# A reordered front and mixer, and inverse roots by Newton's iteration on VectorE

## The chip, the cores and the metric

The kernel runs on one NeuronCore of a Trainium2 chip. A core has five engines with a queue of instructions each: TensorE (PE, matrix products; its weight loads are shown as PEld), VectorE (DVE), ScalarE (ACT), GpSimd (POOL) and SyncE (SP, which mostly starts transfers). Transfers run on 16 DMA engines that all queues share. The metric is the device time of one execution in microseconds.

## The reference

It is one step of a decoder layer for 512 prompt tokens and 32 sample tokens (8 requests of 4). One input projection feeds two groups of heads: retention (q, k, v and a gate; a state of 128 x 128 per head is carried over chunks of 128 tokens) and a causal depthwise convolution of width 31. Both are normed, joined and projected (the mixer); then comes a layer norm. The second half retrieves, for each token and each of 8 heads, 16 of 16384 single-neuron experts by product keys. Cut to what matters:

```python
x = layer_norm(ALPHA * x + mix, ln1_g, ln1_b)           # mix = [silu(g) * head_norm(o), conv_out] @ w_out
q = (x @ w_query).reshape(T, 8, 256)                    # two halves of 128 a head
s1, s2 = q1 . sub_keys_1, q2 . sub_keys_2               # 128 keys each
v1, i1 = top_k(s1, 16); v2, i2 = top_k(s2, 16)
sv, ci = top_k(v1[:, None] + v2[None, :], 16)           # 16 experts a head
gate = softmax(sv); act = gelu(peer_u[idx] . x)
ffn = sum(gate * act * peer_v[idx])
y = layer_norm(ALPHA * x + ffn, ln2_g, ln2_b)
```

Every norm needs 1 / sqrt(var + 1e-5): head norms four values a token, layer norms one.

## The kernel before, in words

All arithmetic is float32 but for the gate tables. The tokens stand in groups: 128 lead tokens, then 416 others (32 samples, a prompt group "b" of 128, and 256 further tokens).

The **lead** goes first through the whole front: projections, `rope`, `conv`, `conv_norm`, retention (`scores`, `attend`, `head_norm`, `gate_heads`), the mixer (`mix_mm`, `mix_norm`) and `retrieve`, the top-k of its queries. After that its 128 gathers can start (`gather`, L568 to L587): a gather fetches 128 rows of 8 KB, one per token, by GpSimd (L573); VectorE takes the dot product with the token (L576), ScalarE the gelu and the weight (L580, L581), and VectorE adds the weighted row to an accumulator (L586). Three buffers hold gathers, and a fourth takes each fourth one.

Beside these gathers runs the **front of the others**: `glu`, `conv` (half on TensorE, half on VectorE, L269), the value projection, `rope` of q and k, three retention chunks, `conv_norm`, then the mixer. In the mixer `mix_a` makes the products of a token group and `mix_b` its layer norm, the transposes to columns (L487) and, for the first two groups, a copy to DRAM (L738). The tokens' columns are `x1T`. `caches` then writes the convolution caches (ten transfers).

Then come the **remaining queries**: four units of 32 products each (two heads a unit, 416 columns wide, L803), their top-k in `retrieve` (its first operation on VectorE is L504), and beside them the **expert scores** (`scores_of`, L781 to L788): for each of 128 blocks of 128 experts, 512 KB are loaded (L784) and multiplied with 256 token columns. Scores of 76 blocks are kept before the gate tables are built (`build`, `first_keys`). At the end `v_stage` multiplies the tables with the experts' other rows (L919, L925, the banks `pB`), while 160 gathers for the samples and group "b" run beside it, and two layer norms close the kernel. The 256 loads of expert blocks alternate between the queues of SyncE and ScalarE (`turns`, L774).

What sets the order of the work: the program is written in the order above, but a scheduler then gives each engine a fixed order of its own by an estimated timeline, with the program order as priority; operations of gathers, norms and projections are interleaved by it. On the chip each engine works its list in order and waits for semaphores. Buffers are rings of tiles: the weights have four of 1 MB (`wp`), the expert blocks four of 512 KB (`uvp`). PSUM has eight banks; in the front five belong to `ps` and three to `ps0`.

An inverse root (`rsqrt`, L182) is two operations of GpSimd: an addition of epsilon and a power of -0.5. GpSimd starts the gathers too. There are 15 such roots: five head norms and ten layer norms.

Of the kernel before, what the change touches and what calls it, by code (L numbers as in the profile page):

```python
# [20 lines left out]
D = 1024  # L21
# [73 lines left out]
def tile_step(ctx: ExitStack, tc: tile.TileContext, a, o):  # L95
# [14 lines left out]
    ps = front.enter_context(tc.tile_pool(name="ps", bufs=5, space=PSUM, reuse_waits="tile"))  # L110
    ps0 = front.enter_context(tc.tile_pool(name="ps0", bufs=3, space=PSUM, reuse_waits="tile"))
# [65 lines left out]
    mhalf = per.tile([128, 1], F32, name="mhalf")  # L177
    G.memset(mhalf, -0.5)
# [3 lines left out]
    def rsqrt(dst, var):  # L182

        G.tensor_scalar(dst, var, EPS, None, op0=OP.add)
        G.tensor_tensor(dst, dst, mhalf[:dst.shape[0]].to_broadcast(list(dst.shape)), op=OP.pow)
# [56 lines left out]
    def silu_gate(w, xT, n, outs, table):  # L242
        for m in range(4):
# [41 lines left out]
    def conv_norm(y, n):  # L285
# [10 lines left out]
        rs = small("ropeB", [128, 416], bufs=1)  # L296
# [21 lines left out]
    def head_norm(po, n, kind):  # L318
# [12 lines left out]
        on = small("on", [128, 512])  # L331
# [11 lines left out]
    def k_tokens(kT, c0, n, kind):  # L343
        pt = mmps()
        kt = small("ktok", [128, 512], bufs=1)
# [7 lines left out]
    def scores(qT, kT, c0):  # L353
# [3 lines left out]
        sc = small("sc", [128, 512])  # L357
# [289 lines left out]
    lastk = rope(load_win(1), 1, xT0, 160, 0, both(k0, kS))  # L647
    conv_norm(y0, 128)
# [3 lines left out]
    silu_gate(load_win(3), xT0, 160, both(g0, gS), True)  # L652
# [101 lines left out]
    for _ in range(KX):  # L754
        next(gather0)
# [277 lines left out]
```

## Time and profile before

| | us |
|---|---|
| three runs | 1593.02, 1601.89, 1602.20 |
| median | 1601.89 |
| the profiled execution | 1610.35 |
| its span in the profile | 1608.6 |
| TensorE busy in it | 1481.2 |
| VectorE busy in it | 1223.1 |

Times in the profile are microseconds from the start of the span. A row of the timeline gives the start, the duration, the engine, the line, the operation, what it writes and reads, how often, and in brackets how long the engine was idle before it and what ended that. A row of the table of groups gives the count, the busy time, the mean duration in ns, and the idle time before the group with what ended it. A row of the table of stretches gives the stretch, its length, the busy time of TensorE, its weight loads, VectorE, ScalarE and GpSimd with the number of instructions, the granted TensorE clock, the share of the DMA engines that was busy, and GB/s.

### The profile page before, as it was taken

How to read it: one execution, taken by the hardware profiler on the slowest of the kernel's cores; microseconds unless marked ns; L12 is line 12 of the kernel's file. 1: busy time of each engine (PE TensorE's matmuls, PEld its weight loads, DVE VectorE, ACT ScalarE, POOL GpSimd, SP SyncE). 2: the span in 40 equal slices, each digit the busy share in tenths (PEclk: the TensorE clock that was granted, in tenths of full speed). 3: DMA queues.
4: the chain of work that ended last, by engine and by line, in shares of the span. 5: the costliest groups of instructions: out<-in, count | busy, mean ns of one | idle time of the engine just before them, and what ended most of it. 6: DMA issues, size and time to landing. Idle time of an engine off the chain costs nothing.

```text
span 1608.6 us, 20726 instructions
## 1 busy us (share of the span) xinstructions
PE 1481.2 (92%) x7014; PEld 1016.0 (63%) x7014; DVE 1223.1 (76%) x3158; ACT 601.6 (37%) x1687; POOL 394.4 (25%) x335
## 2 busy tenths in 40 slices
PE   6899989996879997999999997989999999999997
PEld 6788557554666666888888885434566655644443
DVE  3939989989774999999866989667777677776642
ACT  2225352244221323333623799512994111111100
POOL 1001323433431222221122100233223223333200
PEclk9999989997989999999999997999999999999999
DMA  9458678997789768998699721989999999999972
GB/s 356 178 200 350 247 252 294 345 356 253 262 338 360 254 232 311 351 333 313 221 390 375 282 80 58 374 344 417 375 350 387 418 406 420 416 423 424 425 263 94
DMA packets 99542, 503.75 MB, mean 313 GB/s; under 512 B 10183, under 2 KB 21191, under 8 KB 56549
## 3 DMA queue, kind: packets, MB, share of 16 engines
q0 software_dynamic: 42240, 305.12, 48.9%
q1 hardware_dynamic: 32317, 122.84, 20.5%
q10 hardware_dynamic: 24880, 74.47, 12.4%
q8 instruction: 55, 0.90, 0.2%
q14 instruction: 50, 0.41, 0.1%
HBM read 497.03 MB, written 5.80 MB: 313 GB/s over the span
## 4 chain that ended last, share of the span: by engine, by line
PE 32%; DMA 28%; DVE 20%; issue 12%; POOL 5%; ACT 2%; ACTq 0%; POOLq 0%; SPq 0%; DVEq 0%
DMA g<-in_uv_dram,Ib 15%; PE pB L925 12%; PE sp L787 9%; DMA g<-in_uv_dram,I 8%; DVE acc L586 5%; PE mm L199 5%; POOL g L573 4%; DVE g L576 3%; PE mm L878 2%; DMA uv<-in_uv_dram 2%; DMA g<-in_w_in_dram 2%; DVE score L506 1%; PE mm L309 1%; PE mm L476 1%; DVE iu L505 1%
## 5 line engine op out<-in xcount | busy, mean ns | idle before, releaser
L787 PE MATMUL sp<-x1T,uv 128*128 128x256 f32 x2048 | 465.9, 383 | 25.4 <-DMA uv<-in_ut_dram 13.1
L787 PEld LDWEIGHTS sp<-x1T,uv 128*128 128x128 f32 x2048 | 386.0, 191 | 99.1 <-issue 27.7
L586 DVE SCALAR_TENSOR_TENSOR acc<-g,wgt,acc 128x1024 f32<-128x1024 f32 x285 | 364.8, 1280 | 102.1 <-ACT wgt L581 101.3
L573 POOL DMA_INDIRECT g<-in_uv_dram,I x128 | 177.1, 1384 | 451.9 <-DVE acc L586 253.5
L580 ACT ACTIVATE act<-act 128x1 f32<-128x1 f32 x288 | 57.8, 201 | 611.5 <-DVE g L576 599.9
L573 POOL DMA_INDIRECT g<-in_uv_dram,Ib x128 | 158.2, 1236 | 431.7 <-DVE acc L586 238.0
L576 DVE SCALAR_TENSOR_TENSOR g<-g,x1g 128x1024 f32<-128x1024 f32 x160 | 195.6, 1224 | 89.1 <-DMA g<-in_uv_dram,Ib 60.5
L576 DVE SCALAR_TENSOR_TENSOR g<-g,x 128x1024 f32<-128x1024 f32 x128 | 155.4, 1215 | 38.2 <-DMA g<-in_uv_dram,I 38.0
L199 PE MATMUL mm<-x1T,w 128*128 128x384 f32 (+1 forms) x512 | 177.6, 503 | 0.0
L925 PE MATMUL pB<-uv,Ga 128*128 128x512 f32 x352 | 157.2, 594 | 4.5 <-DMA uv<-in_uv_dram 4.4
L865 ACT ACTIVATE off<-row,e1T 128x128 bf16<-128x128 bf16 x512 | 157.7, 388 | 1.6 <-PE sp L787 0.6
L199 PEld LDWEIGHTS mm<-x1T,w 128*128 128x128 f32 x512 | 97.5, 192 | 71.9 <-issue 39.5
L925 PE MATMUL pB<-uv,Gb 128*128 128x512 f32 x256 | 117.4, 613 | 6.1 <-DMA uv<-in_uv_dram 5.6
L925 PEld LDWEIGHTS pB<-uv,Ga 128*128 128x128 f32 x352 | 66.3, 190 | 77.2 <-issue 67.4
L925 PE MATMUL pB<-uv,Gd 128*128 128x512 f32 x256 | 111.0, 593 | 2.9 <-DMA uv<-in_uv_dram 2.9
L925 PEld LDWEIGHTS pB<-uv,Gd 128*128 128x128 f32 x256 | 48.3, 190 | 65.4 <-issue 60.5
L925 PEld LDWEIGHTS pB<-uv,Gb 128*128 128x128 f32 x256 | 48.7, 196 | 64.2 <-issue 55.3
L878 PEld LDWEIGHTS <-A 128*128 128x128 bf16 x1536 | 64.4, 99 | 35.3 <-issue 26.3
L878 PE MATMUL mm<-B,A 128*128 128x96 bf16 (+1 forms) x1536 | 67.8, 196 | 11.6 <-DVE Gc L904 10.0
L873 DVE TENSOR_TENSOR B<-M,gtT 128x768 bf16<-128x768 bf16 (+1 forms) x192 | 69.5, 418 | 11.6 <-PE mm L878 11.6
L925 PE MATMUL pB<-uv,Gc 128*128 128x512 f32 x160 | 73.0, 601 | 0.0
L867 ACT ACTIVATE A<-off 128x1024 bf16<-128x1024 bf16 x64 | 67.4, 1053 | 14.4 <-PE mm L878 10.3
(279 smaller groups left out, 1701.5 us busy)
## 6 DMA issues: line engine op xcount, KB each, us to landing
uv<-in_ut_dram ACTq DMA_DIRECT2D x80, 512.0 KB
uv<-in_uv_dram SPq DMA_DIRECT2D x80, 512.0 KB
uv<-in_ut_dram SPq DMA_DIRECT2D x48, 512.0 KB
uv<-in_uv_dram ACTq DMA_DIRECT2D x48, 512.0 KB
w<-in_w_in_dram SPq DMA_DIRECT2D x18, 1024.0 KB
w<-in_w_query_dram SPq DMA_DIRECT2D x16, 1024.0 KB
w<-in_w_out_dram SPq DMA_DIRECT2D x7, 1024.0 KB
g<-in_uv_dram,I POOLq DMA_INDIRECT x128, 8.0
```

Source lines behind the costliest of these rows:

```text
L199: T.matmul(p[:, :n], w[m // 2][:, k, (m % 2) * 128:(m % 2 + 1) * 128], xT[:, k, c0:c0 + n], start=(k == 0), stop=(k == 7))
L309: mm = T.matmul(p[:n, q * 256:(q + 1) * 256], xT[:, k, c0:c0 + n], w[q][:, k, :], start=(k == 0), stop=(k == 7))
L573: G.indirect_dma_start(out=t, out_offset=None, in_=a["uv"], in_offset=bass.IndirectOffsetOnAxis(ap=idx[:, k:k + 1], axis=0))
L576: dot = V.scalar_tensor_tensor(t[:, :D], t[:, :D], 1.0, x1, op0=OP.mult, op1=OP.mult, accum_out=act[:, 0:1])
L580: S.activation(act[:, 1:2], act[:, 0:1], AF.Gelu)
L586: V.scalar_tensor_tensor(acc, v, wgt, acc, op0=OP.mult, op1=OP.add)
L787: T.matmul(sp, u[:, k], x1T[:, k, NG2:], start=(k == 0), stop=(k == 7))
L865: S.activation(off[:, t], row, AF.Abs, bias=e1T[:, t1 + t:t1 + t + 1])
L867: S.activation(A, off, AF.Relu, bias=1.0, scale=-1.0)
L873: V.tensor_tensor(B[:, q], M, pairs_of(gtT[:, q], t1).to_broadcast([128, TB // 2, ne, 2]), op=OP.mult)
L878: T.matmul(pt[:, t % nt], A[:, t - t1], B[:, q, (t - t1) // 2, :, t % 2], start=(q == 0), stop=(q == 2))
L925: T.matmul(pB[b][q], W[:, b * 128:(b + 1) * 128], vt[:, q * 512:(q + 1) * 512], start=False, stop=(e == NK - 1), skip_group_check=True)
```

## The change

Four things are changed.

1. `rsqrt` runs on VectorE: epsilon is added, a first guess is made by integer operations on the float's bits, and three rounds of Newton's iteration follow, three operations each, 12 in all. GpSimd's two operations go.
2. The front is reordered. In the lead the gate projection stands ahead of `conv_norm`. For the others, `conv_norm` and `caches` stand ahead of the projection of k; scores and tokens of k are made for all three chunks first, into free tiles; then each chunk's `attend`, `advance` and `head_norm` follow one of four parts of the gate projection. The third block of output weights goes into the convolution's buffer and the second of query weights into the buffer of q and k.
3. The mixer gets four new PSUM banks (`mx`), and the first query unit four others (`pq`). That unit is computed in three passes over its columns, as the token groups are normed, and no longer after the mixer. The norm of the first prompt group stands ahead of the products of the second, not behind them.
4. All loads of expert blocks are in SyncE's queue.

```diff
+    fps = ExitStack()
+    ps = fps.enter_context(tc.tile_pool(name="ps", bufs=5, space=PSUM, reuse_waits="tile"))
+    ps0 = fps.enter_context(tc.tile_pool(name="ps0", bufs=3, space=PSUM, reuse_waits="tile"))
...
     def rsqrt(dst, var):
-        G.tensor_scalar(dst, var, EPS, None, op0=OP.add)
-        G.tensor_tensor(dst, dst, mhalf[:dst.shape[0]].to_broadcast(list(dst.shape)), op=OP.pow)
+        tmp = gw.tile([128, 2, H], F32, name="nwt")
+        x, t = (tmp[:dst.shape[0], i, 0:dst.shape[1]] for i in range(2))
+        V.tensor_scalar(x, var, EPS, None, op0=OP.add)
+        V.tensor_scalar(dst.bitcast(I32), x.bitcast(I32), 1, None, op0=OP.logical_shift_right)
+        V.tensor_scalar(dst.bitcast(I32), dst.bitcast(I32), -1, 0x5F3759DF, op0=OP.mult, op1=OP.add)
+        for _ in range(3):
+            V.tensor_tensor(t, dst, dst, op=OP.mult)
+            V.scalar_tensor_tensor(t, t, -0.5, x, op0=OP.mult, op1=OP.mult)
+            V.scalar_tensor_tensor(dst, t, 1.5, dst, op0=OP.add, op1=OP.mult)
...
+    silu_gate(load_win(3), xT0, 160, both(g0, gS), True)
     conv_norm(y0, 128)
     sc = scores(q0, k0, 0)
     po = attend(0, sc, q0, v0, 0)
     on = head_norm(po, C, "p")
-    silu_gate(load_win(3), xT0, 160, both(g0, gS), True)
     gate_heads(on, C, g0, 0)
...
-    rope(load_win(1), 1, xT, n - NS, 160, [(0, n - NS, kT)])
-    wg = load_win(3)
-    banks[:] = [ps0]
-    ons = {}
-    def retain(c):
-        c0 = C * (c - 1)
-        sc = scores(qT, kT, c0)
-        kt = k_tokens(kT, c0, C, "p")
-        po = attend(c, sc, qT, vs[c], c0)
-        advance(c, kt, vs[c])
-        ons[c] = head_norm(po, C, "p")
-    retain(1)
-    retain(2)
-    banks[:] = [ps]
-    silu_gate(wg, xT, n - NS, [(0, n - NS, gT[:, :, r])], False)
-    wo = load_w(a["w_out"], 0) + load_w(a["w_out"], 512)
+    wk_, wg = load_win(1), load_win(3)
     S.activation(y[:, :, s_], yS, AF.Copy)
     conv_norm(y, n)
+    caches()
+    rope(wk_, 1, xT, n - NS, 160, [(0, n - NS, kT)])
+    spare = [u_p.rearrange("p m t -> p (m t)")[:, 0:2 * D], blk[:, 0:2 * D]]
+    spare = [t.rearrange("p (k e) -> p k e", k=8) for t in spare]
+    wo = load_w(a["w_out"], 0) + load_w(a["w_out"], 512, [spare[0], None])
+    banks[:] = [ps0, ps]
+    flat = lambda t: t.rearrange("p a b -> p (a b)")
+    scs = [None, None, flat(small("qe", [128, 4, 128], bufs=1))]
+    kts = [None] + [flat(small("dg", [128, 4, 128])) for _ in range(2)]
+    for c in range(3):
+        scs[c] = scores(qT, kT, C * c, scs[c])
+        kts[c] = k_tokens(kT, C * c, C, "p", kts[c])
+    ons = {}
+    gate_part = lambda m: silu_gate(wg, xT, n - NS, [(0, n - NS, gT[:, :, r])], False, [m])
     S.activation(gT[:, :, s_], gS, AF.Copy)
-    banks[:] = [ps, ps, ps0, ps, ps0, ps, ps, ps0]
+    for c in range(1, 4):
+        gate_part(c - 1)
+        po = attend(c, scs[c - 1], qT, vs[c], C * (c - 1))
+        advance(c, kts[c - 1], vs[c])
+        ons[c] = head_norm(po, C, "p", bv[0] if c == 3 else None)
+    gate_part(3)
+    wq0 = load_w(a["w_query"], 0, [None, spare[1]])
...
-    gate_heads(ons[1], C, gT, NS)
-    gate_heads(ons[2], C, gT, NS + C)
-    retain(3)
-    gate_heads(ons[3], C, gT, NS + 2 * C)
+    for c in range(1, 4):
+        gate_heads(ons[c], C, gT, NS + C * (c - 1))
+    fps.close()
+    leftp, mxs = ExitStack(), ExitStack()
+    pq = leftp.enter_context(tc.tile_pool(name="pq", bufs=4, space=PSUM, side="right", reuse_waits="tile"))
+    mx = mxs.enter_context(tc.tile_pool(name="mx", bufs=4, space=PSUM, reuse_waits="tile"))
+    banks[:] = [mx]
+    q_first = [pq.tile([128, 512], F32, name="mm") for _ in range(4)]
+    def first_unit(c0, c1):
+        for m in range(4):
+            for k in range(8):
+                T.matmul(q_first[m][:, c0:c1], wq0[m // 2][:, k, (m % 2) * 128:(m % 2 + 1) * 128], x1T[:, k, c0:c1],
+                         start=(k == 0), stop=(k == 7), skip_group_check=True)
     mix_a(0, NS, None)
     mix_a(NS, C, 0)
     mix_b(0, NS)
+    mix_b(NS, C)
     mix_a(NS + C, C, 1)
-    mix_b(NS, C)
     mix_a(NS + 2 * C, C, None)
+    first_unit(0, NS + C)
     mix_b(NS + C, C)
+    first_unit(NS + C, NS + 2 * C)
     mix_b(NS + 2 * C, C)
-    caches()
+    first_unit(NS + 2 * C, n)
...
-        next(turns).dma_start(u, a["ut"][e])
+        nc.sync.dma_start(u, a["ut"][e])
...
-        w = load_w(a["w_query"], h0 * 256)
+        w = load_w(a["w_query"], h0 * 256) if h0 else None
         for m in range(4):
-            S.activation(qs[:, h0 * 2 + m], project(w, m, x1T, 0, n), AF.Copy)
+            S.activation(qs[:, h0 * 2 + m], project(w, m, x1T, 0, n) if h0 else q_first[m][:, :n], AF.Copy)
...
-        next(turns).dma_start(vt, a["uv"][e * NK:(e + 1) * NK, D:])
+        nc.sync.dma_start(vt, a["uv"][e * NK:(e + 1) * NK, D:])
```

More of the change, by code (lines that the diff above doesn't have):

```diff
@@ L1 @@
 from contextlib import ExitStack
-from itertools import cycle
 import numpy as np
@@ L240, in glu, with silu_gate @@
                                        sg[:, c].rearrange("p (b i) -> p b i", b=SB), op0=OP.add, op1=OP.mult)
-    def silu_gate(w, xT, n, outs, table):
-        for m in range(4):
+    def silu_gate(w, xT, n, outs, table, blocks=range(4)):
+        for m in blocks:
             p = project(w, m, xT, 0, n)
@@ L295, in conv_norm @@
             T.matmul(pv[:, :n], onesm, sq[:, :n], start=(m == 0), stop=(m == 3))
-        rs = small("ropeB", [128, 416], bufs=1)
+        rs = small("sg", [128, 416], bufs=1)
         S.activation(rs[:, :n], pv[:, :n], AF.Sqrt, bias=eps_c)
@@ L330, in head_norm @@
         V.scalar_tensor_tensor(nb[:n], mv[:n, :, 0], -1.0, rs[:n], op0=OP.mult, op1=OP.mult)
-        on = small("on", [128, 512])
+        if on is None:
+            on = small("on", [128, 512])
         for h in range(H):
@@ L351, in k_tokens, with scores @@
         return kt
-    def scores(qT, kT, c0):
+    def scores(qT, kT, c0, sc=None):
         pa = mmps()
@@ L755, in tile_step @@
         next(gather0)
+    mxs.close()
     front.close()
@@ L765, in tile_step @@
     sel[0] = left.enter_context(tc.tile_pool(name="sel", bufs=2))
-    leftp = ExitStack()
-    pq = leftp.enter_context(tc.tile_pool(name="pq", bufs=4, space=PSUM, reuse_waits="tile"))
     banks[:] = [pq]
```

15 lines of the change are left out of this document (6 added, 9 removed).

## The prediction

> **What bounds the kernel now.** I read the busy line of the page first, then a table of stretches that I cut where the work changes: the lead chunk, the retrieval of that chunk with the convolution, the stretch M (rest of the front and the mixer), the remaining queries, the expert scores, the building of gate tables, the products with gathers beside them, and the end.
>
> ```profile
> span 1608.6 us, 20726 instructions
> PE 1481.2 (92%) x7014; PEld 1016.0 (63%) x7014; DVE 1223.1 (76%) x3158; ACT 601.6 (37%) x1687; POOL 394.4 (25%) x335
> core 0: us, PE busy (x) PEld busy (x) DVE busy (x) ACT busy (x) POOL busy (x), PEclk, DMA share, GB/s
> 0.00:111.00 111.00, 89.40 (x528) 79.96 (x528) 67.58 (x272) 25.83 (x64) 10.12 (x21) 0.95 0.65 242
> 111.00:312.40 201.40, 190.87 (x863) 133.41 (x862) 175.89 (x503) 79.83 (x210) 60.80 (x40) 0.97 0.82 295
> 312.40:515.90 203.50, 170.48 (x734) 122.83 (x733) 151.51 (x247) 67.08 (x168) 68.57 (x59) 0.91 0.84 315
> 515.90:810.00 294.10, 279.17 (x1251) 219.76 (x1250) 278.48 (x1090) 110.71 (x279) 66.06 (x53) 0.99 0.79 288
> 810.00:875.00 65.00, 64.86 (x319) 56.66 (x319) 38.82 (x52) 14.28 (x51) 14.59 (x14) 1.00 1.01 403
> 875.00:1050.00 175.00, 162.47 (x1242) 119.48 (x1242) 146.13 (x455) 137.34 (x385) 19.41 (x18) 0.94 0.56 205
> 1050.00:1531.00 481.00, 458.51 (x1934) 255.06 (x1933) 341.24 (x507) 160.45 (x523) 151.61 (x124) 0.99 0.99 402
> 1531.00:1608.60 77.60, 65.47 (x152) 28.79 (x152) 23.43 (x36) 6.12 (x13) 3.28 (x7) 0.96 0.48 170
> ```
>
> TensorE is busy for 1481 of 1609 us, and its work is nearly the same in both kernels. So the time is that work plus TensorE's idle time, 127 us in all, and the change is worth what it does to those 127. They lie at 21.6 us in the lead, 10.5 to the end of the convolution, 33.0 in M, 15.1 up to 875 us, 12.5 in the building, 22.5 beside the gathers and 12.1 at the end. From 810 to 875 us TensorE is busy 64.86 of 65 us: it is what the gate tables wait for, so a delay of TensorE before that point passes on whole.
>
> M runs from the last convolution operation on VectorE to the first top-k operation of the remaining queries (of the rows with an arrow, the numbers are the total wait in us, how many, the longest):
>
> ```profile
> 311.80 0.60 DVE L269 SCALAR_TENSOR_TENSOR blk<-u_p,cols,blk 128x384 f32<-128x384 f32 x1
> 515.95 0.29 DVE L504 MAX8 vf<-score 128x8 f32<-128x128 f32 x1 [5.53 <-ACT score L525]
> PE mm L340 <- ACT on L333: 13.3, 2, 11.8
> PE mm L487 <- DVE xr L456: 10.5, 1, 10.5
> PE mm L487 <- DVE lrs L452: 5.9, 1, 5.9
> 478.52 22.71 PE L199 MATMUL mm<-x1T,w 128*128 128x416 f32 x64
> 501.08 13.98 PE L787 MATMUL sp<-x1T,uv 128*128 128x256 f32 x64
> ```
>
> The waits of TensorE in M are for norms: 13.3 us for a head norm, 10.5 and 5.9 for layer norms. These are the holes that the change is aimed at. After them come the first query unit (22.71 us) and 13.98 us of expert scores, in which VectorE has little to do.
>
> **The change, part by part.**
>
> *The gathers in M.* The scheduler writes a fixed order for each engine, and VectorE's order holds the two operations of every expert gather (a dot product and an accumulation) between the operations of the norms. In the emitted orders, M holds 44 dots and 46 accumulations before, and 61 and 62 in the changed kernel: 95 dots instead of 80 are ahead of the first top-k. The mixer waits for VectorE in that order, so their cost counts.
>
> ```profile
> L586 DVE SCALAR_TENSOR_TENSOR acc<-g,wgt,acc 128x1024 f32<-128x1024 f32 x46 | 58.8, 1278 | 17.9 <-ACT wgt L581 17.5
> L576 DVE SCALAR_TENSOR_TENSOR g<-g,x 128x1024 f32<-128x1024 f32 x44 | 53.5, 1218 | 21.9 <-DMA g<-in_uv_dram,I 21.9
> DVE acc L586 <- ACT wgt L581: 17.5, 12, 8.7
> DVE lrs L452 <- POOL lrs L185: 5.3, 3, 2.2
> 359.87 0.16 DVE L326 TENSOR_TENSOR hrs<-hmv,cst 128x4 f32<-128x4 f32 x1
> 359.95 0.61 DVE L253 SCALAR_TENSOR_TENSOR blk<-mm,cols,sg 128x384 f32<-128x384 f32 x1
> 71.59 0.29 DVE L282 TENSOR_TENSOR tap_s<-u_s,cols 128x128 f32<-128x128 f32 x1
> 71.91 0.29 DVE L283 TENSOR_TENSOR samples<-samples,tap_s 128x128 f32<-128x128 f32 x1
> ```
>
> A tiny operation keeps VectorE for 0.08 us of its 0.16 when the next one does not need its result (359.87 to 359.95). With the same overlap a dot costs 1.14 us and an accumulation 1.20. The extra work is 17 x 1.14 + 16 x 1.20 = 38.6 us.
>
> *Newton's iteration.* Each inverse root was two GpSimd operations and is now 12 tiny ones on VectorE; 92 of them stand in M. At 0.08 us that is 7.4 us; if each had to wait for the one before, as the pair at 71.59 and 71.91 does at 0.32 us apart, 29 us. I take 7.4, since the order puts gather operations and other norms between most of them, and keep the other end for the range. What goes is the 5.3 us for which VectorE waited on GpSimd, and GpSimd's queue now holds gathers alone.
>
> VectorE's work in M is then 151.5 + 38.6 + 7.4 = 197.5 us, against 203.5 us that M lasts today. VectorE idled 39.8 us beside the gathers in M; without one wait of 8.7 us for ScalarE, that is 0.7 us for each of the 44. Zero idle gives 197.5 us, 0.7 for each of 61 gathers gives 240. I take 0.5, as the denser order has fewer other norms to wait for but the same four gather buffers: M = 197.5 + 30.5 = 228 us, **24.5 us longer**.
>
> *First query unit by columns.* It becomes three passes over the same weights, with 160, 128 and 128 columns, and starts while later token groups are still being normed. Such narrow products stand in the lead:
>
> ```profile
> 80.75 7.70 PE L199 MATMUL mm<-g,w 128*128 128x160 f32 x48
> 111.10 2.05 PE L199 MATMUL mm<-g,w 128*128 128x128 f32 x16
> ```
>
> The wide pass has 64 records. The narrow ones make 64 x 0.160 + 128 x 0.128 = 26.7 us, 4 more than the 22.7 in M today. I add nothing, because without the scores TensorE has 170.5 - 14 = 156.5 us of work in M and 228 - 156.5 = 71 us of holes; uncovered it would be the 4. With only four PSUM banks left for the mixer, the norm of the first prompt group now stands directly ahead of the next product, where it was covered by half a product. What M no longer holds are the 13.98 us of expert scores: in the emitted order the first top-k products follow the query unit at once. That work comes later, on TensorE, **14 us**.
>
> *Lead and convolution.* The gate projection (32 products) moves ahead of the convolution norm, where TensorE waited for VectorE:
>
> ```profile
> PE mm L209 <- DVE ropeB L211: 3.6, 2, 3.4
> PE mm L289 <- DVE g L269: 2.0, 1, 2.0
> ```
>
> That can return up to 5.6 us; I take 4, as two Newton roots (24 operations, 2 us or more) join that chain. From there to M, VectorE has two gathers fewer ahead of it, about 5 us in a stretch where it is 87% busy; I take 4. Together **-8**, bounds 0 and -12.
>
> *After M.* VectorE has 15 gathers (35 us) fewer between 516 and 810 us, and the 80 expert loads that stood in ScalarE's queue go to SyncE's. TensorE's waits there are
>
> ```profile
> PE sp L787 <- ACT Ga L833: 9.7, 5, 3.7
> PE sp L787 <- ACT Gb L838: 2.4, 3, 0.9
> ACT qs L803 <- DMA out_dram<-on: 10.1, 1, 10.1
> ```
>
> I take **-8** of those 12.1, bounds 0 and -15. The ten cache outputs, issued earlier on SyncE, no longer hold the query copies for 10.1 us; TensorE was doing scores meanwhile, so by itself this is worth nothing. On SyncE they now stand among the output-projection loads, with the third block waiting for the convolution buffer; these loads have the whole retention to land, and I cost them at nothing. Without that cover the mixer would wait for one load of 1 MB, some 3 us at 315 GB/s. The half of the query weights that goes into the query buffer waits for the last chunk's products, which precede the mixer by 60 us of TensorE work: nothing. The 48 expert-row loads that join SyncE are weighed among the rivals.
>
> *The end.* Two norms follow the last product:
>
> ```profile
> 1595.81 0.21 DVE L449 BATCH_NORM_AGGREGATE lmv<-lst 128x2 f32<-128x12 f32 x1
> 1597.41 0.14 DVE L452 SCALAR_TENSOR_TENSOR lrs<-lmv,lrs 128x1 f32<-128x1 f32 x1
> ```
>
> From statistics to scale took 1.6 us through GpSimd; twelve operations take 1.0 to 3.9 us by the two spacings above. I take **+1** (bounds -0.5 and +3).
>
> **Sum**: -8 + 24.5 + 14 - 8 + 1 = +23.5 us. The profiled execution took 1610.35 us, span 1608.6; it would take 1634. The runs shown have a median of 1601.89 (1593 to 1602), so I forecast **1625 us**. A change of under 1%, 16 us, cannot be told from none by a measurement of this kernel.
>
> **The rivals.**
>
> *VectorE keeps pace.* If gathers land early enough that VectorE hardly idles in M, M is 197.5 us and the sum is -8 - 6 + 14 - 8 + 1 = -7: **1595 us**. It speaks for this that GpSimd issues gathers as soon as a buffer is free; against it, that VectorE idled 52 us in M with fewer gathers. The order breaks even at 204.5 us, 3.35 us a gather.
>
> *The loads are the gain, and the kernel is faster.* Beside the gathers TensorE waits 21.1 us for expert loads:
>
> ```profile
> PE pB L925 <- DMA uv<-in_uv_dram: 10.8, 8, 4.0
> PE sp L787 <- DMA uv<-in_ut_dram: 10.3, 9, 2.3
> q0 software_dynamic: 17484, 127.39, 64.4%
> q1 hardware_dynamic: 9100, 33.14, 18.0%
> q10 hardware_dynamic: 8928, 32.51, 16.8%
> ```
>
> Half of them are issued from ScalarE's queue, behind its arithmetic. If late issue is their cause, SyncE starts each as its buffer falls free and most of the 21 us go; with M at 205 us the sum is 0.5 - 17 = -17: **1585 us**, and with M at 197.5, 1578. It decides only if M stays under about 205 us. Against it: the transfer engines are 99% busy in that stretch, so the loads are late because the path is full.
>
> [...]
>
> **How the numbers follow.** Forecast 0.55, with a range of its own from 1605 to 1640 (idle of 0.2 to 0.7 us a gather, and the bounds of the other terms). VectorE keeps pace 0.20 (1587 to 1609). Faster by the loads 0.12. One queue starves 0.13. Left out of 1588 to 1655 are the faster case, a little of the second, and the top of the last, together under 0.2; dependent Newton operations, up to 22 us more, fall inside it. Slower than 1618: 0.13 and seven tenths of 0.55. Faster than 1586: 0.12 and 0.03 of the second. The rest is within 1%.
>
> **What would show it.** In the changed profile the first top-k of the remaining queries should begin near 304 + 228 = 532 us (502 if VectorE keeps pace), with 95 dots before it, TensorE some 70 us idle since the convolution, and its waits for VectorE's norms longer, not gone. From there to the gate tables TensorE should idle under 10 us. [...] I am wrong if M is under 205 us, or if TensorE's idle time before 875 us shrinks.

## The result and the profile after

The changed kernel takes **1662.62 us** (median of four runs, 1653.63 to 1667.79) against 1602.05 of the kernel before: a ratio of **1.0386, with a 95% interval of 1.0331 to 1.0441**. It is slower by 61 us of the medians, 48 of the profiled executions (1658.23 against 1610.35, spans 1656.5 and 1608.6).

The busy line of the page of the changed kernel, and its table of stretches, cut at the same events as the prediction's table:

```profile
span 1656.5 us, 21212 instructions
PE 1501.9 (91%) x7142; PEld 1022.3 (62%) x7142; DVE 1244.7 (75%) x3338; ACT 603.1 (36%) x1686; POOL 351.4 (21%) x304
core 0: us, PE busy (x) PEld busy (x) DVE busy (x) ACT busy (x) POOL busy (x), PEclk, DMA share, GB/s
0.00:111.00 111.00, 90.25 (x551) 80.38 (x552) 70.31 (x296) 27.61 (x68) 7.91 (x16) 0.97 0.67 249
111.00:302.20 191.20, 181.37 (x817) 126.04 (x816) 169.94 (x498) 73.99 (x193) 47.75 (x36) 0.97 0.81 296
302.20:554.40 252.20, 175.45 (x820) 131.14 (x821) 201.49 (x392) 75.96 (x200) 86.32 (x61) 0.80 0.81 305
554.40:790.00 235.60, 227.35 (x1013) 176.82 (x1013) 230.38 (x1029) 83.83 (x193) 39.16 (x33) 1.00 0.72 260
790.00:895.00 105.00, 102.81 (x495) 89.84 (x494) 64.69 (x89) 34.76 (x114) 26.73 (x24) 1.00 0.97 382
895.00:1070.00 175.00, 163.73 (x1289) 129.67 (x1288) 122.92 (x420) 122.44 (x350) 9.80 (x9) 0.95 0.45 159
1070.00:1580.00 510.00, 496.59 (x2019) 260.63 (x2018) 360.28 (x548) 179.04 (x559) 133.69 (x127) 0.99 1.00 396
1580.00:1656.50 76.50, 64.34 (x149) 27.77 (x147) 24.64 (x69) 5.51 (x11) 0.00 (x0) 0.95 0.42 149
```

M, from the last convolution operation to the first top-k of the remaining queries, is 252.2 us in place of 203.6. TensorE idles 76.75 us in it (before: 33.0), and its granted clock is 0.80 (before: 0.91).

| | before | predicted | after |
|---|---|---|---|
| convolution ends | 312.4 | 304 | 302.2 |
| first top-k | 516.0 | 532 | 554.4 |
| M | 203.6 | 228 | 252.2 |
| first top-k to the first operation on table Gb | 354.7 | 360.7 | 359.5 |
| from there to the end | 737.9 | 739 | 742.6 |

So the difference is M: +48.6 of 47.9 us in all. The terms around it cancel: -10.2, +4.8, +4.7.

What TensorE and VectorE waited for in M of the changed kernel (total us, how many, the longest):

```profile
PE mm L495 <- DVE keys L464: 26.1, 2, 17.3
PE mm L495 <- DVE xr L464: 12.7, 1, 12.7
PE mm L363 <- DVE blk L218: 11.6, 3, 7.2
PE mm L346 <- ACT on L339: 10.1, 1, 10.1
PE mm L346 <- ACT b_v L339: 6.7, 1, 6.7
DVE g L584 <- DMA g<-in_uv_dram,I: 37.5, 26, 5.5
```

L495 is the transposes behind a layer norm, L346 those behind a head norm: TensorE stands before norms for 55.6 of the 76.75 us, against 29.7 before. Why the norms are late is seen in VectorE's own order. These are operations of one head norm of the changed kernel (L331 takes the variance, L184 to L186 are the first three of the root, L333 uses the finished root), with some of what stands between them:

```profile
380.32 0.15 DVE L331 TENSOR_TENSOR hrs<-hmv,cst 128x4 f32<-128x4 f32 x1
...
382.70 1.23 DVE L584 SCALAR_TENSOR_TENSOR g<-g,x 128x1024 f32<-128x1024 f32 x1 [1.31 <-DMA g<-in_uv_dram,I]
...
384.05 1.28 DVE L594 SCALAR_TENSOR_TENSOR acc<-g,wgt,acc 128x1024 f32<-128x1024 f32 x1
385.24 0.17 DVE L184 TENSOR_SCALAR nwt<-hrs 128x4 f32<-128x4 f32 x1
...
386.31 1.27 DVE L594 SCALAR_TENSOR_TENSOR acc<-g,wgt,acc 128x1024 f32<-128x1024 f32 x1
387.50 0.17 DVE L185 TENSOR_SCALAR hrs<-nwt 128x4 int32<-128x4 int32 x1
...
387.86 1.20 DVE L584 SCALAR_TENSOR_TENSOR g<-g,x 128x1024 f32<-128x1024 f32 x1
388.98 0.08 DVE L584 DVE_READ_ACCUMULATOR g<-g,x 128x1 f32 x1
388.98 0.17 DVE L186 TENSOR_SCALAR hrs<-hrs 128x4 int32<-128x4 int32 x1
...
401.75 0.16 DVE L333 TENSOR_TENSOR hrs<-hrs,cst 128x4 f32<-128x4 f32 x1
```

From the variance to the use of the root it takes 21.4 us, with twelve operations of 0.16 us in between. Eleven gather operations of 1.2 us stand in nine of the thirteen gaps of this chain and fill some 13 us of it; operations of another head norm, of the gate projection (L258) and of the retention (L388), and 1.5 us of waiting for a gather, fill most of the rest. With the power, in the kernel before, the norms from 279 us on took 1.5 to 6.3 us each.

### The profile page after: what moved, and what is told of

The parts are those of the page before. It is cut to its first block, busy times and chain, and to the rows that moved or that the text cites. A ratio compares the mean times of both kernels' runs of the same rounds, so it can differ in the third digit from the quotient of the medians.

```text
span 1656.5 us, 21212 instructions
## 1 busy us (share of the span) xinstructions
PE 1501.9 (91%) x7142; PEld 1022.3 (62%) x7142; DVE 1244.7 (75%) x3338; ACT 603.1 (36%) x1686; POOL 351.4 (21%) x304
## 4 chain that ended last, share of the span: by engine, by line
PE 37%; DMA 25%; DVE 22%; issue 10%; POOL 4%; ACT 2%; SPq 0%; POOLq 0%; DVEq 0%; ACTq 0%
PE sp L808 16%; PE pB L946 13%; DMA uv<-in_ut_dram 7%; DMA g<-in_uv_dram,I 7%; DVE acc L594 5%; POOL g L581 4%; DVE g L584 4%; DMA uv<-in_uv_dram 3%; DMA g<-in_uv_dram,Ib 3%; PE mm L204 3%; PE mm L899 2%; DMA g<-in_uv_dram,Is 2%; DMA g<-in_w_in_dram 2%; PE mm L764 1%; DVE iu L513 1%
## 5 line engine op out<-in xcount | busy, mean ns | idle before, releaser
L808 PE MATMUL sp<-x1T,uv 128*128 128x256 f32 x2048 | 461.1, 381 | 14.3 <-ACT Ga L854 9.8
L581 POOL DMA_INDIRECT g<-in_uv_dram,I x128 | 171.7, 1342 | 531.8 <-DVE acc L594 235.4
L581 POOL DMA_INDIRECT g<-in_uv_dram,Ib x128 | 136.9, 1070 | 518.0 <-DVE acc L594 330.2
L946 PE MATMUL pB<-uv,Ga 128*128 128x512 f32 x352 | 162.4, 604 | 1.2
L204 PE MATMUL mm<-x1T,w 128*128 128x384 f32 (+1 forms) x448 | 157.7, 508 | 0.7 <-DVE sc L366 0.7
L204 PEld LDWEIGHTS mm<-x1T,w 128*128 128x128 f32 x448 | 86.6, 195 | 63.5 <-issue 32.6
```

The costliest lines, as they stand in the source:

```text
L204: T.matmul(p[:, :n], w[m // 2][:, k, (m % 2) * 128:(m % 2 + 1) * 128], xT[:, k, c0:c0 + n], start=(k == 0), stop=(k == 7))
L581: G.indirect_dma_start(out=t, out_offset=None, in_=a["uv"], in_offset=bass.IndirectOffsetOnAxis(ap=idx[:, k:k + 1], axis=0))
L808: T.matmul(sp, u[:, k], x1T[:, k, NG2:], start=(k == 0), stop=(k == 7))
L946: T.matmul(pB[b][q], W[:, b * 128:(b + 1) * 128], vt[:, q * 512:(q + 1) * 512], start=False, stop=(e == NK - 1), skip_group_check=True)
```

## The experiments

In the table, "norms" is the time from the variance to the operation that uses the root, summed over the four head norms and four layer norms from 279 us on; "dots" is how many gather dot products stand ahead of the first top-k in VectorE's emitted order. The kernel before had medians of 1600 to 1602 us beside these runs. M, norms and dots are of one profiled execution each; those of e4 and e5 are the slowest of their runs. M does not hold the same work everywhere: in the kernel before, e7 and e14 it has 64 products of expert scores, 14 us, which come behind it in the changed kernel, e2 to e4, e10 to e13, e15 and e16 (at most 2 are left in M there). The others have 32 to 56.

| kernel | us | ratio, 95% | M | norms | dots |
|---|---|---|---|---|---|
| before | 1602 | | 203.6 | 32 | 80 |
| changed | 1662.62 | 1.0386 (1.0331-1.0441) | 252.2 | 127 | 95 |
| e1 Newton alone | 1655.72 | 1.0341 (1.0292-1.0390) | 249.2 | 160 | 92 |
| e2 changed, power | 1635.41 | 1.0194 (1.0140-1.0248) | 216.2 | 38 | 88 |
| e3 changed, dots from 75 held | 1644.00 | 1.0268 (1.0215-1.0320) | 226.4 | 107 | 80 |
| e4 changed, dots from 61 held | 1645.73 | 1.0265 (1.0215-1.0314) | 209.4 | 92 | 66 |
| e5 Newton alone, one round | 1642.65 | 1.0244 (1.0209-1.0279) | 236.4 | 110 | 88 |
| e6 square root and reciprocal | 1624.76 | 1.0114 (1.0049-1.0180) | 207.8 | 46 | 82 |
| e7 before, one queue | 1599.55 | 0.9981 (0.9961-1.0001) | 203.4 | 32 | 80 |
| e8 before, dots from 61 held | 1600.91 | 0.9992 (0.9966-1.0018) | 180.8 | 24 | 68 |
| e9 Newton alone, guarded | 1620.81 | 1.0116 (1.0071-1.0161) | 215.9 | 88 | 80 |
| e10 changed, power, old mixer | 1613.37 | 1.0068 (1.0042-1.0093) | 206.0 | 32 | 85 |
| e11 changed, power, unit whole | 1628.27 | 1.0162 (1.0124-1.0199) | 219.5 | 34 | 89 |
| e12 as e11, old mixer order | 1614.93 | 1.0099 (1.0063-1.0134) | 205.9 | 34 | 85 |
| e13 changed, guarded | 1621.78 | 1.0137 (1.0104-1.0170) | 218.0 | 72 | 81 |
| e14 before, guarded | 1608.55 | 1.0046 (1.0023-1.0068) | 209.6 | 26 | 80 |
| e15 changed, power, guarded | 1611.77 | 1.0067 (1.0044-1.0090) | 208.4 | 23 | 80 |
| e16 as e10, guarded | 1616.89 | 1.0115 (1.0076-1.0154) | 203.6 | 25 | 80 |

**Which part costs: Newton's iteration alone (e1), and the rest without it (e2).** e1 puts the new `rsqrt` into the kernel before; e2 takes it out of the changed kernel again:

```diff
     def rsqrt(dst, var):
-        tmp = gw.tile([128, 2, H], F32, name="nwt")
...
+        G.tensor_scalar(dst, var, EPS, None, op0=OP.add)
+        G.tensor_tensor(dst, dst, mhalf[:dst.shape[0]].to_broadcast(list(dst.shape)), op=OP.pow)
```

> The kernel before with Newton's iteration alone; front, mixer and queues as before. Its emitted order has 34 dots of gathers ahead of the last convolution operation and 92 ahead of the first top-k of the remaining queries, so 58 in stretch M (44 before, 61 in the changed kernel). Theory 1, that VectorE's order with too many gathers in M makes the loss: M grows by 14 x (2.34 + 0.9) + 7 = 52 us to about 255 us, the time to 1645 to 1655 us. Theory 2, that the reordered mixer with its uncovered norms makes the loss and Newton costs only its own 92 small operations: 1605 to 1612 us.

> The changed kernel with GpSimd's power in place of Newton's iteration; the rest as changed. Its order has 36 dots ahead of M and 88 at its end, so 52 in M. Theory 1: M shrinks from 252 us by 9 x 3.3 + 7 to about 215 us, the time from 1662 to about 1625 us. Theory 2: the mixer is still the changed one, 1650 to 1658 us.

M of e1, and two of TensorE's waits in it; below them M of e2:

```profile
306.50:555.70 249.20, 176.54 (x726) 122.29 (x725) 194.59 (x383) 75.42 (x198) 90.76 (x59) 0.83 0.83 311
```

```profile
PE mm L345 <- ACT on L338: 27.0, 2, 22.7
PE mm L492 <- DVE nwt L189: 20.7, 1, 20.7
```

```profile
313.40:529.60 216.20, 168.56 (x816) 127.88 (x817) 168.48 (x270) 69.98 (x177) 82.57 (x66) 0.86 0.85 317
```

Newton's iteration alone makes the kernel 54 us slower, nearly all that the whole change does; one wait of 20.7 us is put down to an operation of the iteration itself (L189). But without it 33 us stay. In both runs M came out near theory 1 (about 255 and 215 us); the time of e2 is 10 us above it and fits neither theory. The two parts do not add up to 61: each by itself makes the mixer's norms late (the aggregate of the last one is at 512.9 us in e1, at 505.8 in e2 and at 466.2 in the kernel before).

**Is it the gathers' number in M? (e3, e4)** In the changed kernel the later dots are kept behind the mixer's last norm:

```diff
+            if x1 is x1_0 and k >= 74:
+                behind(dot, held[0])
```

In e4 the number is 60.

> The changed kernel, with the dots of gathers 75 and later kept behind the last norm of the mixer in the order. It has 34 dots ahead of M and 80 at its end: 46 in M, as many as before (44), but the mixer, its banks and Newton's iteration are the changed ones. Theory 1: M about 208 us, the time 1615 to 1625 us. Theory 2: M stays above 235 us, the time above 1645 us.

> As the run with 74, but the dots of gathers 61 and later are kept back: 32 in M, 66 ahead of the first top-k. Theory 1: M is then no longer bound by gathers but by TensorE's products and the norms, 175 to 190 us; later VectorE has 14 more gathers between the top-k operations than before, which may cost 5 to 10 us; the time 1590 to 1605 us. Theory 2: above 1645 us.

Both theories missed a part. M falls by 26 and 43 us, and the layer norms are short again (2.4 to 2.6 us in e4), but only 17 to 19 us are gained, and e4 gains no more than e3: what is put off comes back as work later (from the first top-k to the end e4 takes 1134 us, the changed kernel 1102). In both kernels the head norms are as stretched as ever (39, 22, 16 us).

**How the cost goes with the chain's length (e5, e6).** In the kernel before, one round in place of three (six operations; the roots are less exact), or a ScalarE square root and a VectorE reciprocal:

```diff
-        for _ in range(3):
+        for _ in range(1):
```

```diff
+        S.activation(dst, var, AF.Sqrt, bias=eps_c[:dst.shape[0]])
+        V.reciprocal(dst, dst)
```

> The kernel before with Newton's iteration in place of GpSimd's power, but one round in place of three: six dependent VectorE instructions a norm in place of twelve (the roots are less exact; nothing else is left out). Theory 'stretched chain': what costs is that gather instructions of about 1.2 us are put between the dependent ones, so the cost goes by their number; the stretch M, which twelve lengthened by 46 us, should grow by 18 to 28 us (222 to 232 us), and the time should come to 1622 to 1632 us. Rival 'another order': the cost is not in the chain's length but in the order that the whole kernel is given once the root leaves GpSimd; then six cost what twelve do, M near 249 us and 1650 to 1658 us.

> The kernel before with the root as one ScalarE square root and one VectorE reciprocal: GpSimd is out of the norms as with Newton's iteration, but the chain has one VectorE instruction. 'Stretched chain': the norms take 3 to 6 us each, as with the power, so M is 198 to 210 us and the time 1597 to 1610 us. 'Another order': once GpSimd is out, M is near 249 us and the time 1645 us or more.

M is 203.6, 207.8, 236.4 and 249.2 us for no, one, six and twelve dependent VectorE operations: it goes with the chain, and GpSimd's absence alone (e6) does little to M. The dots ahead of the first top-k go with it too (80, 82, 88, 92), so these runs by themselves do not part the chain's length from the number of gathers; e3 and e13 do, below. Six operations cost more than half of what twelve cost (41 us against 54), so my proportional estimate missed. The time of e6 is 15 us above the range that I had for it, though M is in its range. Of the 12.5 us between the two profiled executions 4.2 lie in M, 5.4 ahead of it and 5.5 beside the later gathers. What costs them is not shown; ScalarE is busy 634.1 us in e6 against 601.6, and 13 table loads of 1.28 us stand at the line of the square root:

```profile
L182 ACT ACT_TABLE_LOAD x13 | 16.7, 1283 | 3.3 <-DVE x L662 2.9
```

**One queue, and holding dots back in the kernel before (e7, e8).** e7 changes `next(turns).dma_start` to `nc.sync.dma_start` at both places; e8 is the edit of e4 in the kernel before.

> The kernel before with every expert load of the scoring and building stages issued by SyncE, as the changed kernel has it, and nothing else. If one queue paces the loads a little slower, as the last 610 us of the changed kernel lasting 6 us longer suggest: 1605 to 1610 us, all of the difference behind the first gate-table multiplication. The rival from the prediction, one queue starves the loads: 1615 us or more with waits for loads of 20 us. If the queue is nothing and those 6 us are the gather's: 1600 to 1603 us.

> The kernel before with the gather's dot products from the 60th on kept behind the mixer's last norm (the order alone changes). If gather instructions ahead of the mixer's norms already cost in the kernel before, and what is put off finds room later: M falls from 204 us to 185 to 193 us and the time to 1588 to 1596 us. If VectorE has no room later, as the two holds of the changed kernel suggest (17 us less of M, nothing of the time): M falls by 8 to 15 us, the scoring and building stages give it back, and the time is 1600 to 1610 us.

TensorE's waits for expert loads between the gate tables and the last dot, in the kernel before, in e7 and in the changed kernel:

```profile
PE pB L925 <- DMA uv<-in_uv_dram: 12.8, 10, 4.0
PE sp L787 <- DMA uv<-in_ut_dram: 10.3, 9, 2.3
```

```profile
PE pB L923 <- DMA uv<-in_uv_dram: 2.5, 2, 1.5
PE sp L785 <- DMA uv<-in_ut_dram: 1.7, 1, 1.7
```

```profile
PE sp L808 <- DMA uv<-in_ut_dram: 3.6, 21, 0.2
PE pB L946 <- DMA uv<-in_uv_dram: 2.0, 4, 0.8
```

One queue takes 19 us of waits away and neither costs nor wins time (0.9961 to 1.0001). e8 takes 23 us off M, more than either theory had, and wins nothing: from the first top-k to the end it takes 18 us longer. That is the second theory, that VectorE has no room later.

**The same instructions with the chains kept together (e9, e13).** An order constraint holds each dot behind the norm that it should not come ahead of. Nothing else is changed, and all twelve operations run. `roots` are the last operations of the roots in program order; in e13 the counts are 31, 48, 51, 56, 64, 67, 72, 80:

```diff
+        roots.append(end)
...
+            if x1 is x1_0 and k >= 31:
+                behind(dot, roots[max(j for j, c in {2: 31, 3: 48, 4: 51, 5: 57, 6: 64, 7: 65, 8: 69, 9: 73}.items() if c <= k)])
```

> The kernel before with Newton's iteration alone (three rounds, twelve instructions), and an order constraint: from the 31st on, the gather's dot products may not come ahead of the norms that they stand behind in the kernel before (31 ahead of the first later norm, 48, 51 and 57 ahead of the prompt's head norms, 64, 65, 69 and 73 ahead of the mixer's norms). So the same twelve instructions run, with few gather instructions between them. 'Stretched chain': the head norms take 4 to 9 us in place of 29 to 43, M is 205 to 220 us and the time 1605 to 1622 us. If Newton's own work or the loss of GpSimd's order is what costs: M over 235 us and 1640 us or more.

> The changed kernel whole, Newton's iteration in it, with the order constraint on the gather's dot products alone (31 ahead of the first later norm, 48, 51 and 56 ahead of the head norms, 64, 67, 72 and 80 ahead of the mixer's). If the stretched chains are what Newton's iteration costs here too, it comes to what the changed kernel gives with the power back, 1635 us, and something for the chains that stay partly stretched (the same constraint on the kernel before left 18 us): 1632 to 1648 us, M 214 to 232 us. If something else in the iteration costs: M over 240 us and 1652 us or more.

M of e13, and the head norm of the same chunk as above (the first, the last and some of its twelve operations):

```profile
296.60:514.60 218.00, 170.42 (x831) 127.52 (x831) 176.91 (x358) 68.36 (x177) 61.36 (x48) 0.87 0.79 299
```

```profile
366.58 0.16 DVE L334 TENSOR_TENSOR hrs<-hmv,cst 128x4 f32<-128x4 f32 x1
366.77 0.17 DVE L186 TENSOR_SCALAR nwt<-hrs 128x4 f32<-128x4 f32 x1
366.98 0.17 DVE L187 TENSOR_SCALAR hrs<-nwt 128x4 int32<-128x4 int32 x1
...
368.76 0.16 DVE L191 SCALAR_TENSOR_TENSOR nwt<-nwt 128x4 f32<-128x4 f32 x1
368.96 0.16 DVE L192 SCALAR_TENSOR_TENSOR hrs<-nwt,hrs 128x4 f32<-128x4 f32 x1
```

With nothing between them the twelve take 2.4 us in place of 16.5 (385.24 to 401.72 in the changed kernel). Three dots follow them here, so from the variance to the use of the root it is 5.9 us in place of 21.4. The constraint wins 35 us for Newton's iteration alone and 41 for the whole change; e13 came out 10 us under the range that I had for it. But the expectation of e9 was missed in one point: its head norms take 6.9 to 22 us, not 4 to 9, so the chains are kept together only in part.

e3 is the fair comparison for the reason. It has as many dots ahead of the top-k as e13 (80 and 81) and layer norms as long in sum (22 us both), but head norms of 84 us in place of 50, and it takes 22 us longer. In the two profiled executions 8.3 of 23.3 us of this lie in M, 7.8 ahead of it and 5.7 beside the later gathers, so it is not shown that the norms make all of it.

**Controls (e14, e15): the same constraint with the power.** Here the dots stand behind the first VectorE operation that uses the root.

> The kernel before, power and all, with the order constraint of the guarded Newton kernel (31, 48, 51, 57, 64, 65, 69, 73), here ahead of the first VectorE operation that uses the root. It is the control of that run: what the constraint does without Newton's iteration. If the constraint helped there only by keeping gather instructions out of Newton's chains: 1596 to 1604 us here, and the whole 35 us there belong to the chains. If spreading the gather thinner helps by itself: 1570 to 1590 us, and Newton's part is larger than the 18 us that stayed.

> The changed kernel with GpSimd's power back and the same order constraint as the guarded changed kernel (31, 48, 51, 56, 64, 67, 72, 80). If the constraint also helps the reordered mixer, whose norms wait for VectorE directly: 1605 to 1618 us, M near 205 us, and Newton's iteration with guarded chains costs some 5 to 15 us. If it helps Newton's chains only: 1630 to 1638 us as without it; then Newton's iteration, guarded, would be no cost, but a gain of 10 us.

e14 is slower than both of its theories had it: in the old order the constraint by itself costs 6.5 us. e15 is where its first theory had it: in the changed order the constraint wins 24 us without Newton's iteration.

| us | gathers free | gathers guarded |
|---|---|---|
| before | 1602.05 | 1608.55 |
| before, Newton | 1655.72 | 1620.81 |
| changed, power | 1635.41 | 1611.77 |
| changed (Newton) | 1662.62 | 1621.78 |

With the gathers guarded (the counts differ a little between the two orders), Newton's iteration costs 12 us in the old order and 10 in the new one, and the rest of the change 3 and 1. With the gathers free the same parts cost 54 and 27, 33 and 7. So most of the loss is neither in the new instructions nor in the new order of the stages, but in where the scheduler puts gather instructions once a norm's chain has gaps or the mixer leaves VectorE waiting. The constraint moves gathers out of the chains and out of M alike (80 and 81 dots in place of 88 to 95), and the square does not part the two. The guarded chains are still not all short (88 and 72 us of norms, against 26 and 23), so the 10 to 12 us are no clean price of the iteration.

**What of the reordering costs (e10, e11, e12).** All three are e2 with more of the mixer undone: e10 has the whole old mixer (eight banks, old order, query unit behind it), e11 only the unit whole, e12 the unit whole and the old order, with the four banks kept. This is the edit of e12:

```diff
     mix_b(0, NS)
-    mix_b(NS, C)
     mix_a(NS + C, C, 1)
+    mix_b(NS, C)
     mix_a(NS + 2 * C, C, None)
-    first_unit(0, NS + C)
     mix_b(NS + C, C)
-    first_unit(NS + C, NS + 2 * C)
     mix_b(NS + 2 * C, C)
-    first_unit(NS + 2 * C, n)
+    first_unit(0, n)
```

> The changed kernel with GpSimd's power back, and its mixer as in the kernel before: eight PSUM banks for it in place of four, the old order of its four blocks, and the first query unit whole behind it, from weights loaded there. What stays of the change is the front's order (gates between the heads' blocks, scores and keys ahead, cache writes early) and the one queue. Theory 'mixer': the 34 us that stayed with the power back come from the four banks and the columns: 1600 to 1612 us. Theory 'front': they come from the front's order: 1625 to 1640 us, with the conv end to the first mixer norm as long as with the power back alone (116 us).

> The changed kernel with GpSimd's power back and the first query unit computed whole behind the mixer's last norm, from the weights and into the banks that the change gives it; only the column pieces are undone (192 matmuls of 128 to 160 columns, 27 us with the power back, in place of 64 of 416). If the pieces cost by their own work: TensorE's busy time falls by 5 us and the time is 1626 to 1632 us. If they pay by filling the wait for the mixer's norms: M grows by 10 to 20 us and the time is 1640 to 1655 us.

> The changed kernel with GpSimd's power back, the first query unit whole, and the mixer's four blocks in the old order; the four PSUM banks for the mixer stay, and so do the front and the one queue. It stands between the run with the unit whole (1628 us, M 219.5 us) and the one with the old mixer altogether (1613 us, M 206 us). Theory 'order': what cost those 15 us is that two blocks' matmuls stand ahead of the third norm: 1611 to 1618 us. Theory 'banks': it is the four banks for eight: 1625 to 1631 us.

It is the order: 13 us between the medians of e11 and e12 (their slowest and fastest runs, 1619.12 and 1627.08 us, are still 8 apart), nothing more for the banks (1614.93 and 1613.37, intervals overlapping). The statistics of the mixer's norms in e11 and e12 (first and last start):

```profile
L451 DVE BATCH_NORM_STATS2 lst<-mm x6: 678/690/694, 429.6 to 489.9; 128x6 f32<-128x512 f32 x6
```

```profile
L451 DVE BATCH_NORM_STATS2 lst<-mm x6: 678/688/693, 429.4 to 474.1; 128x6 f32<-128x512 f32 x6
```

The first begins at the same time; the last is 16 us later in e11. TensorE's rows show where these 16 us arise, first e11, then e12:

```profile
445.37 1.09 PE L490 MATMUL mm<-cst,keys 128*128 128x128 f32 x4 [13.53 <-DVE keys L459]
```

```profile
447.73 1.04 PE L490 MATMUL mm<-cst,keys 128*128 128x128 f32 x8
```

These are the transposes of the first prompt group. In the new order they stand ahead of the products of the second group, and TensorE waits 13.5 us for their norm; in the old order those products fill the wait. So it is this wait, and not the products of two groups ahead of the third norm, as my theory had it. Of the 13 us it can be all; four more dots (89, against 85) stand ahead of the first top-k in e11 too. The column pieces by themselves are 7 us, with overlapping intervals, so not told from nothing. What stays of the change in e10 and e12, the front's order and the one queue above all, leaves 11 and 13 us over the kernel before.

**A version from all this (e16):** e10 with the constraint.

> The changed front and the one queue with the old mixer and the power (1613 us without the constraint), and the order constraint added: every part that the runs found to cost is out. If the constraint gives what it gave to the changed kernel, 10 us or more: 1595 to 1605 us, level with the kernel before or a little ahead. If it gives nothing without long chains: 1610 to 1616 us.

It gains nothing, and is a little slower than the range for that (1610 to 1616 us). No kernel of these was faster than the one before by more than its interval.

## Why the prediction was wrong

The direction and the place were right: slower, and in M. The forecast of 1625 us was 38 us low, and 1663 lies above the range's end of 1655. Of these 38 us, 24.4 are in the sum, 47.9 between the profiled executions in place of 23.5. Another 8.5 come from setting the sum on the median of the kernel before, which lies that much under its profiled execution, and 4.4 from the changed kernel's profiled execution, which lies under its own median.

- **M = VectorE's work + idle per gather: the step that failed.** The work was foreseen, 197.5 us against 201.49, and the 61 dots too. The idle time was not. "I take 0.5" made it 30.5 us, and it was 50.7, 0.83 a gather: 20 of the 24 us by which M is over 228. In the kernel before, VectorE idles 203.5 - 151.5 = 52.0 us in M; the 0.5 let 21 us of this go. VectorE's waits for ScalarE's weights did shrink (from 17.5 to 7.9 us), but its waits for gathers that had not landed grew (from 21.9 to 37.5). Nor does the idle time go by the number of gathers: in 17 of the 18 profiles it is 41 to 61 us, with 32 to 61 dots in M (in e4 it is 74). The rule misses e2, which has no Newton's iteration, by as much: 168.5 + 0.5 x 52 = 194.5 us, against 216.2. With the 52.0 us kept, M would have been forecast at 249.5 us and the time at 1647. Why the whole stays near 50 us is open.
- **Newton's iteration, 7.4 us.** As time for which the chain keeps VectorE this is about right: from e2 to the changed kernel VectorE's work in M grows by 33.0 us, of which nine dots and ten accumulations are 22.3, and 10.7 are left for the 92 operations. As the cost of the iteration it is far too little. "I take 7.4, since the order puts gather operations and other norms between most of them": the observation is right, the conclusion the wrong way round. What stands between two dependent operations hides the 0.20 us at which they follow each other alone (e13), and costs 1.2 us instead, and TensorE waits for the chain's end. I had the additional gathers in another term (38.6 us) and did not see that about half of them come with the iteration (52 dots in M in e2, 61 with it). Measured: 54 us alone, 27 on top of the rest, 10 to 12 with the dots guarded. The upper bound, 29 us, used the 0.32 us of larger operations; the small ones of e13 follow each other in 0.20, which makes 18.
- **TensorE's holes in M** were foreseen at 71 us and are 76.75. That these agree while M is 24 us longer is in part luck: TensorE's busy time in M is 175 us, where I counted 156.5 without the scores and up to 4 for the narrower unit. One reason is that 20 more products of 384 columns lie in M (128 in place of 108, 47.0 us in place of 37.4). The other is that products last longer: e15, which has nearly the same products in M, shows TensorE busy 164.3 us at a granted clock of 0.88, the changed kernel 175 at 0.80.
- **"Its work is nearly the same in both kernels"** fails by 20.7 us of TensorE's busy time. The parts show where they come from. One queue alone (e7) makes it 12.9 us longer, and TensorE's idle time 18.9 shorter. Newton's iteration alone (e1) makes it 10.1 us longer, and with the dots guarded (e9) it is as before (1480.9 us). The groups of the transposes behind the layer norms, changed kernel first:

```profile
L495 PE MATMUL mm<-cst,keys 128*128 128x128 f32 x16 | 4.3, 426 | 26.8 <-DVE keys L464 26.1 <-DVE lmv L457 0.7
```

```profile
L487 PE MATMUL mm<-cst,keys 128*128 128x128 f32 x16 | 2.1, 273 | 0.0
```

  The same products take 426 ns behind waits of up to 17 us and 273 ns without a wait, and the granted clock in M is 0.80 against 0.91. Around the longest of these waits, from the first transposes to the next ones, it is 0.50:

```profile
460.20:478.30 18.10, 0.85 (x9) 0.74 (x8) 14.16 (x32) 4.37 (x14) 5.97 (x5) 0.50 0.78 268
```

  No run changes the clock alone, so how much of the longer products goes with it is not shown.
- **The order of the mixer**, priced at nothing: "the norm of the first prompt group now stands directly ahead of the next product, where it was covered by half a product". The place was right, the price was not. TensorE waits 17.3 us there in the changed kernel (the longest of the waits for L464) and 13.5 in e11, and the order costs 13 us with the power (e12 against e11).
- **The scores (+14) and what follows M (-8)** were foreseen as +6 together and measured +4.8; TensorE idles 10.4 us there, against "under 10".
- **Lead and convolution, -8:** this profile shows -10.2. But the convolution's end varies between profiles of the same front: 300.9 to 321.0 us in the eight with the old one (mean 310.3), 296.6 to 313.4 in the ten with the new one (mean 304.7). By these means the term is nearer to -5.5.
- **The query unit, 0 (4 if uncovered):** 7 us at most (e11), within what the runs can't tell.
- **The end, +1:** from the last gather dot to the end it is 65.1 us before and 68.6 after, +3.5. The two norms there, from the aggregate to the scale, went from 1.6 and 1.5 us to 3.6 and 2.6; but e7, with the power, shows 68.7 for the same stretch, so the iteration is not shown to be the cause.
- **The rivals.** "VectorE keeps pace" needed M at 197.5 us. "One queue starves", with 0.13 of the chances and a share in the range's upper end, is refuted: no run shows a term for starved loads; in its place the waits for loads fell from 23.1 to 5.6 us, and e7 is level (0.9981). "The loads are the gain" was right that one queue ends the waits, from 23.1 to 4.2 us in e7, and wrong that this is worth time.

I did not have the rival that the experiments brought out: that the norms' own latency grows with each operation of the chain that the scheduler can part from the next. The rows for it were there. In the kernel before, a reciprocal of 2.75 us and two gather operations already stood in the gap of the power, from 373.09 to 379.40 us, and that head norm took 6.3 us where the lead's took 1.7.

## What to carry to other kernels

A chain of small dependent instructions on an engine that also does filler work is priced by its gaps, not by its busy time (here 16.5 us for the twelve operations with gathers between them, 2.4 us without): multiply the number of gaps by the length of the filler that the scheduler can put into each, and look at the emitted order for it. Before a hop to another engine is replaced by a chain at home, compare the time from input to result, and where the chain has to stay, try to keep the filler behind it by an order constraint (here worth 35 and 41 us; in the changed order 24 also without the chain, in the old order without the chain a loss of 6.5). When a stretch is added up as work and idle time, keep the idle time that was measured unless something in the change takes it away. Measure parts in a square (each alone, both, and the filler held), since the costs of two edits need not add (here 54 and 33 make 61).

## What the runs showed of the hardware

- An operation of the iteration, on 128x4 elements by VectorE, lasts 0.16 or 0.17 us in the rows of e13. There it starts 0.19 to 0.21 us behind the one whose result it needs (366.77 and 366.98; 368.76 and 368.96). Behind an operation on 128x4 elements whose result it does not need, the next one starts after 0.07 to 0.08 us (380.32 and 380.39 in the changed kernel; 359.87 and 359.95 in the kernel before).
- One load queue in place of two cut TensorE's waits for loads from 23.1 to 4.2 us (e7) beside the gathers, where the transfer engines are 99% busy in the kernel before, at the same time for the kernel (0.9981). The products are recorded longer instead. This is the group of the products with table Ga, of the kernel before and of e7:

```profile
L925 PE MATMUL pB<-uv,Ga 128*128 128x512 f32 x352 | 157.2, 594 | 4.5 <-DMA uv<-in_uv_dram 4.4
```

```profile
L923 PE MATMUL pB<-uv,Ga 128*128 128x512 f32 x352 | 162.4, 604 | 0.1
```

  In this group waiting went over into busy time, 4.4 us against 5.2. Over the groups of all four tables the busy time went from 458.6 to 466.7 us and the idle time from 13.5 to 3.6. Why the products lengthen was not tried.
